# A hybrid encoder block on one core: the order of the first products, of the latent projections and of the retention output

## The chip, the cores and the metric

The kernel runs on one core of one Trainium2 chip. The metric is device time of that core in microseconds (us); lower is better. The time before is the median of three runs.

## The reference, cut to what matters

One encoder layer over 1024 tokens and 16 learned meta tokens, width 1024, all in float32:

```python
u    = rmsnorm(h)
proj = u @ w_in    # rq, rk (512 each), rv, rg (1024 each), a_cq (384), a_ckv (256), a_kr (32), two gates (1024 each)
y_ret = (silu(rg) * group_norm(bidir_retention(rope(rq), rope(rk), rv))) @ w_ret_out      # 8 heads
y_mla = attention(rmsnorm(a_cq) @ w_uq, rmsnorm(a_ckv) @ w_uk, ..w_uv, rope(a_kr)) @ w_mla_out
h = h + (sigmoid(g1) * y_ret + sigmoid(g2) * y_mla) @ w_o
h = h + (silu(n @ w_gate) * (n @ w_up)) @ w_down     # n = rmsnorm(h)
out = rmsnorm(h)[:, 16:]
```

The retention of a head works on chunks of 128 tokens: scores inside a chunk times a decay mask, a state that runs from chunk to chunk (one forward, one backward), and a group norm over the head's 128 outputs.

## The kernel before, in words

**Products.** Activations lie transposed, channels on partitions and tokens along the free axis. A 256-column slice of a projection is made by `seven` (L175), which splits weights and tokens in two halves each and forms a 2 by 2 block product with seven products instead of eight. Their names are 11, t2, t3, n1, 21, t4, 22 (L30). The contraction of 1024 channels goes in four pairs of 128-row blocks, so one product is 4 pairs x 3 matmuls = 12 matmuls of 128x512, and a `seven` has 84. There are three matmuls per pair because every fp32 operand is cut into a high and a low fp32r half, and high x high, high x low and low x high are summed (L208, L209). ScalarE writes the high half (L201 for weights, L260 and L266 for tokens), VectorE the low half (L202, L261, L267). `seven` loads the four weight blocks (L181), GpSimd adds them up (L183 to L185, L199). Products 11 and 21 share PSUM bank a, t3 and t4 bank c, n1 and 22 bank d (L31). `seven_out` (L221) drains the banks into four output blocks.

**The order.** The program is traced in the order of its text, and a scheduler lays out every engine's queue, all DMA triggers on SyncE's (SP's), by a timeline of its own; an instruction can stand in its queue before one that comes earlier in the text. A tile waits until the slot, or the closed pool's memory, that it takes over is free. On the chip each queue runs in order.

**Stage 1, the first products (L286 to L330).** For each of four pairs q the x blocks are loaded, their token blocks derived (L308 VectorE, L310 and L312 GpSimd) and split, and two slices (rg, numbers 0 and 1: `pa`, `pb`) take three or four products of that pair at once. Then x21 comes, t4 (L325) and 22 follow, and both slices are drained. The meta tokens' blocks `um`, `umd` are made after that (L333 to L342).

**Stage 2 (L481 to L492).** Four slices of v (each transposed per chunk, L436), the squares of x for the norm (`squares`, L372, GpSimd adds L380), `input_norm`, `decays` (a 128x128 decay mask per head and row weights, kept in SBUF, L358 to L360), four slices of q and k with rotary tables.

**Stage 3, the retention heads (L498 to L613).** `core_pair` loads and transposes k for two heads (L507). `core` loads v (L522), computes the states (L530 to L542) and then, for one half of the tokens after the other, scores (L552), mask (L554), output y (L558, L559), statistics (L564, L565), a square root on ScalarE (L566), the normalised y (L570), its transpose (L573), the gate (L574) and a store to DRAM tensor `z_d` (L575). Nearly all of a head's tiles have one buffer, PSUM pool `pc` has three banks. After each head a filler, one `seven`, is traced: rg slices 2 and 3, then eight gate slices; two are left after the last head. `z_sums` (L578) makes the derived blocks of `z_d` per pair, reading and writing DRAM.

**Stage 4, latents and the retention output (L614 to L758).** `cc.close()` frees the heads' memory. In it lie the latents `cq`, `ckv` (L618, L619), which stay in SBUF until the attention uses them. `latent_part` (L625) fills them from slices 20 (kv), 21 (q) and 22 (q and rotary key). Then 28 token blocks of Z are loaded from `z_d` and split (L706 to L710), the rotary parts of q are made (L720 to L746), and four slices of the retention output follow (`ret_post`, L748, L758). Attention (from L761), the output projection and the feed-forward layers come after.

## Time and profile before

| | |
|---|---|
| runs, median (lowest to highest) | 1871.55 us (1870.2 to 1873.42) |
| profiled execution, its own time | 1871.53 us |
| its span, first to last instruction | 1869.8 us |
| mean granted TensorE clock | 0.968 |
| DMA | 225.20 MB, 120 GB/s over the span |
| busy: TensorE, VectorE, ScalarE, GpSimd | 1746.0, 1337.9, 902.5, 859.9 us |

The profile is that of one execution. A group of instructions has a line number of the kernel, an engine (PE is TensorE, PEld its weight loads, DVE VectorE, ACT ScalarE, POOL GpSimd, SPq the queue that issues DMAs), the tiles written and read, a count, busy time and mean duration, and behind the second bar the idle time just before its instructions with what ended it. In a line of a timeline the first number is the start, the second the length in us. Matmuls are pipelined: the distance from start to start is what one costs, not its duration. A table of windows gives, for each stretch, its length, then busy time and count of each engine, the granted clock, the busy share of the DMA engines and GB/s.

### The profile page before, as it was taken

The numbers are of one execution on the slowest core, as the hardware profiler recorded it, in microseconds if no ns is written. First come the engines' busy times: TensorE is split into PE (matmuls) and PEld (weight loads), VectorE is DVE, ScalarE is ACT, GpSimd is POOL, SyncE is SP. The second block draws the span as 40 slices with busy tenths as digits, with TensorE's granted clock in tenths as the row PEclk, the third lists the DMA queues.
The fourth block names the chain that finished last, engine by engine and source line by source line (L and its number), as shares of the span: only waits on it lengthen the run. The fifth ranks groups of instructions, "written<-read, shape, count | busy, mean of one in ns | idle before, by whom it ended". The sixth has DMA issues, their size and how long they took to land.

```text
span 1869.8 us, 26307 instructions
## 1 busy us (share of the span) xinstructions
PE 1746.0 (93%) x8821; PEld 1461.1 (78%) x8821; DVE 1337.9 (72%) x2391; ACT 902.5 (48%) x1649; POOL 859.9 (46%) x680
## 2 busy tenths in 40 slices
PE   5799999999995749999999999999999999999998
PEld 3588778888884637889989888778888888777787
DVE  8544687677774676678878775876766666888975
ACT  5443663565442342367777734533323332544435
POOL 4612575675652313223432251567656676432331
PEclk8899999999997869999999999999999999999999
DMA  3622234445342165411101265432233333665422
GB/s 135 207 89 77 96 97 164 142 157 175 133 158 93 47 209 191 148 27 33 39 27 63 85 212 189 136 97 95 96 113 103 107 95 108 213 201 161 147 62 91
DMA packets 127415, 225.20 MB, mean 120 GB/s; under 512 B 16368, under 2 KB 30112, under 8 KB 127280
## 3 DMA queue, kind: packets, MB, share of 16 engines
q1 hardware_dynamic: 127280, 223.52, 36.3%
q8 instruction: 70, 1.15, 0.2%
q14 instruction: 65, 0.53, 0.1%
HBM read 158.64 MB, written 64.76 MB: 119 GB/s over the span
## 4 chain that ended last, share of the span: by engine, by line
PE 78%; DVE 10%; DMA 5%; issue 3%; ACT 2%; POOL 1%; SPq 0%; DVEq 0%; POOLq 0%; ACTq 0%
PE mm L209 51%; PE mm L129 3%; PE mm L130 3%; PE mm L131 3%; PE o L866 3%; PE t L836 2%; DVE slot L146 2%; PE s L129 1%; DVE slot L202 1%; PE s L130 1%; PE s L131 1%; DMA slot<-z_d 1%; DMA slot<-f_d 1%; DMA slot<-in_xT 1%; PE mm L552 1%
## 5 line engine op out<-in xcount | busy, mean ns | idle before, releaser
L209 PE MATMUL mm<-slot,slot 128*128 128x512 f32 x2604 | 597.2, 391 | 10.9 <-DVE slot L202 5.4
L209 PEld LDWEIGHTS mm<-slot,slot 128*128 128x128 f32 x2604 | 489.9, 189 | 117.1 <-DVE slot L202 7.8
L201 ACT CAST slot<-slot 128x512 fp32r<-128x512 f32 (+1 forms) x427 | 254.7, 599 | 471.3 <-PE mm L209 393.2
L202 DVE TENSOR_TENSOR slot<-slot,slot 128x512 fp32r<-128x512 f32 (+1 forms) x427 | 391.7, 919 | 97.8 <-ACT slot L201 89.5
L209 PE MATMUL mm<-ht,slot 128*128 128x512 f32 x648 | 224.5, 407 | 28.9 <-DVE slot L739 23.9
L209 PE MATMUL mm<-h,slot 128*128 128x512 f32 x648 | 228.1, 410 | 18.3 <-ACT slot L201 12.4
L209 PEld LDWEIGHTS mm<-ht,slot 128*128 128x128 f32 x648 | 124.7, 194 | 56.2 <-issue 28.2
L199 POOL TENSOR_TENSOR slot<-slot,slot 128x512 f32<-128x512 f32 (+1 forms) x61 | 83.3, 1365 | 178.3 <-DVE slot L202 144.8
L183 POOL TENSOR_TENSOR slot<-slot,slot 128x512 f32<-128x512 f32 (+1 forms) x61 | 84.8, 1391 | 174.0 <-DVE slot L202 50.2
L209 PEld LDWEIGHTS mm<-h,slot 128*128 128x128 f32 x648 | 125.6, 195 | 46.8 <-ACT slot L201 13.5
L209 PE MATMUL mm<-l,slot 128*128 128x512 f32 x324 | 130.8, 404 | 1.3 <-DVE l L267 1.3
L209 PE MATMUL mm<-lt,slot 128*128 128x512 f32 x324 | 129.8, 401 | 0.1
L146 DVE TENSOR_TENSOR slot<-slot,slot 128x512 fp32r<-128x512 f32 x123 | 107.4, 889 | 14.5 <-ACT slot L145 14.1
L184 POOL TENSOR_TENSOR slot<-slot,slot 128x512 f32<-128x512 f32 (+1 forms) x61 | 80.7, 1323 | 63.2 <-DVE slot L202 61.1
L826 DVE TENSOR_SCALAR_CACHE_REDUCE pr<-s,sq_c 128x384 f32<-128x384 f32 (+1 forms) x192 | 103.4, 574 | 8.8 <-PE t L844 5.4
L145 ACT CAST slot<-slot 128x512 fp32r<-128x512 f32 x123 | 74.7, 620 | 71.2 <-DMA slot<-f_d 29.3
L131 PE MATMUL mm<-slot,slot 128*128 128x512 f32 (+1 forms) x288 | 105.4, 366 | 0.0
L130 PE MATMUL mm<-slot,slot 128*128 128x512 f32 (+1 forms) x288 | 105.4, 366 | 0.0
L129 PE MATMUL mm<-slot,slot 128*128 128x512 f32 (+1 forms) x288 | 105.2, 367 | 0.0
L839 DVE TENSOR_TENSOR ptl<-t,pth 128x512 fp32r<-128x512 f32 x128 | 85.7, 685 | 21.9 <-ACT pth L838 21.2
L185 POOL TENSOR_TENSOR slot<-slot,slot 128x512 f32<-128x512 f32 (+1 forms) x61 | 87.7, 1437 | 1.8
L838 ACT CAST pth<-t 128x512 fp32r<-128x512 f32 x128 | 71.6, 579 | 24.0 <-PE t L836 23.6
(341 smaller groups left out, 3505.2 us busy)
## 6 DMA issues: line engine op xcount, KB each, us to landing
slot<-in_w_in SPq DMA_DIRECT2D x92, 256.0 KB
f_d<-slot SPq DMA_DIRECT2D x71, 256.0 KB
slot<-f_d SPq DMA_DIRECT2D x71, 256.0 KB
slot<-in_xT SPq DMA_DIRECT2D x48, 256.0 KB
slot<-z_d SPq DMA_DIRECT2D x44, 256.0 KB
slot<-in_w_g SPq DMA_DIRECT2D x44, 256.0 KB
slot<-in_w_u SPq DMA_DIRECT2D x44, 256.0 KB
slot<-in_w_dq SPq DMA_DIRECT2D x48, 192.0 KB
```

The source lines that it names most:

```text
L129: pe.matmul(ps, sh, mh, start=start, stop=False)
L130: pe.matmul(ps, sh, ml, start=False, stop=False)
L131: pe.matmul(ps, sl, mh, start=False, stop=stop)
L146: dve.tensor_sub(lo, t, f(hi))
L183: pool.tensor_add(s1, a21, a22)
L185: pool.tensor_sub(a21, a11, a21)
L199: pool.tensor_sub(s2, s2, a12)
L201: act.copy(hi, side[b])
L202: dve.tensor_sub(low, side[b], f(hi))
L209: pe.matmul(ps, sw[:, ks], sx, start=begins and q == qs[0] and i == 0, stop=q == nq - 1 and i == 2, skip_group_check=True)
L826: dve.tensor_scalar(pr[:, c], ps[:, :n], sq_c[:, qb : qb + 1], None, ALU.mult, ALU.max, accum_out=mx[:, j : j + 1])
L839: dve.tensor_sub(pt[1][d], tp, f(pt[0])[d])
```

## The change

1. The first products. Instead of two slices with pair after pair of all products, four slices (0 to 3) get products 11 and 21 first, with the first 512 tokens only. The other token blocks are made meanwhile, the sums on VectorE instead of GpSimd, in a fixed order (`issue_after`). Then `rest_out` drains slices 0 and 1 together, five products each, and slices 2 and 3 one by one; these two are no fillers any more. The four partial products wait in SBUF (`es`). The weight blocks 11 and 21 of the four slices are loaded twice.

```diff
+    t_d = mk(dram, (16, P, P), "t_d")
+    cq_d = mk(dram, (3, 2, P, S), "cq_d")
+    ckv_d = mk(dram, (2, 2, P, L), "ckv_d")
...
-        pool.tensor_sub(a21, a11, a21)
+        pool.tensor_sub(a21, a21, a11)
...
-        bt1 = sb(c1, "tokens", 4)
+        rfill = sb(right, "rfill", 1, side="right")
+        fill(rfill, 32)
+        mid = ExitStack()
+        bta = sb(mid, "tokens_a", 4, side="right")
+        mp = sb(mid, "misc", 1, side="right")
+        btb = sb(c1, "tokens_b", 4)
         wr1, ws1 = sb(c1, "w1r", 5), sb(c1, "w1s", 2)
         wh1, wl1 = sb(c1, "w1h", 3), sb(c1, "w1l", 3)
         cr = sb(c1, "c1", 6)
-        pm = sb(c1, "ps_mm", 5, space=PSUM)
-        pc = sb(c1, "ps_core", 3, space=PSUM)
+        pm = sb(c1, "ps_mm", 4, space=PSUM)
+        pc = sb(c1, "ps_core", 4, space=PSUM)
...
+        places = [bta]
+
+        def block(nm):
+            pl = places[0] if nm in ("11", "t2") else btb
+            return [mk(pl, (P, 512), t + nm, F32R) for t in "hl"]
...
+        def rest_out(group, pl):
+            for prod, e, post in group:
+                dve.tensor_add(e, prod("t2"), e)
+            vs = [slot(pl) for _ in group]
+            for (prod, e, post), v in zip(group, vs):
+                dve.tensor_sub(v, e, prod("n1"))
+            for (prod, e, post), v in zip(group, vs):
+                dve.tensor_add(v, prod("t3"), v)
+                post("22", v)
+            for prod, e, post in group:
+                t = slot(pl)
+                dve.tensor_add(t, prod("t4"), e)
+                post("21", t)
+            for prod, e, post in group:
+                dve.tensor_sub(e, e, prod("22"))
+                post("12", e)
...
         U = [{} for _ in range(4)]
+        cc, a1 = ExitStack(), ExitStack()
+        tb = sb(cc, "tables")
+        hold = sb(a1, "hold", 3)
         with ExitStack() as c2:
-            xp, hold = sb(c2, "x", 7), sb(c2, "hold", 8)
-            wf = sb(c2, "wfirst", 8)
+            xp, wf, wb = sb(c2, "x", 16), sb(c2, "wfirst", 2), sb(c2, "wfirst_r", 3)
...
-            kept = []
-            for q in range(4):
-                w1, w2 = column(C_MIX + 2 * q), column(C_MIX + 2 * q + 1)
-                x11 = xload(2 * q, 0)
-                if q == 0:
-                    pa = seven((wr1, ws1, wf, wf, pm), win(0), U)
-                x12, x22 = xload(2 * q, 1), xload(2 * q + 1, 1)
-                if q == 0:
-                    pb = seven((wr1, ws1, wh1, wl1, pc), win(1), U)
-                g12, n1, g22, t2 = slot(cr), slot(cr), slot(hold), slot(hold)
-                U[q]["11"] = bscale("11", x11, w1)
-                act.mul(g12, x12, w1)
-                dve.scalar_tensor_tensor(n1, x11, w1, g12, ALU.mult, ALU.subtract)
-                act.mul(g22, x22, w2)
-                pool.tensor_add(t2, g22, n1)
-                U[q]["t2"] = bsplit("t2", t2)
-                pool.tensor_sub(g12, g22, g12)
-                U[q]["t3"] = bsplit("t3", g12)
-                U[q]["n1"] = bsplit("n1", n1)
-                for b in NAMES[:3]:
-                    pa(b, [q])
-                    pb(b, [q])
-                pa("n1", [q])
-                kept.append((g22, t2))
-            x21 = [xload(2 * q + 1, 0) for q in range(4)]
-            for q in range(4):
-                U[q]["21"] = bscale("21", x21[q], column(C_MIX + 2 * q + 1))
-            for q in range(4):
-                g22, t2 = kept[q]
-                dve.scalar_tensor_tensor(t2, x21[q], column(C_MIX + 2 * q + 1), t2, ALU.mult, ALU.subtract)
-                U[q]["t4"] = bsplit("t4", t2)
-            for q in range(4):
-                U[q]["22"] = bsplit("22", kept[q][0])
-            seven_out(pa, cr, rg_post(0), {b: () for b in NAMES[:4]})
-            seven_out(pb, cr, rg_post(1), {b: () for b in NAMES[:3]})
...
+            def products(ps, w, b, q, begins):
+                ks = slice(q * P, q * P + P)
+                for i, (sw, sx) in enumerate(((w[0], U[q][b][0]), (w[0], U[q][b][1]), (w[1], U[q][b][0]))):
+                    pe.matmul(ps, sw[:, ks], sx, start=begins and i == 0, stop=q == 3 and i == 2, skip_group_check=True)
...
+            banks = [mk(pm, (P, 512), "mm") for _ in range(4)]
+            x11, x21, wa11, es = [], [], [], []
+            for i in range(4):
+                x11.append(xload(2 * i, 0))
+                wa11.append(wfirst(win(i)[0], wf if i == 3 else wh1, wf if i == 3 else wl1))
+                U[i]["11"] = bscale("11", x11[i], col(2 * i))
+                for q in range(i):
+                    products(banks[i], wa11[i], "11", q, q == 0)
+                for j in range(i + 1):
+                    products(banks[j], wa11[j], "11", i, i == 0)
+            for i in range(4):
+                es.append(slot(hold if i < 3 else cr))
+                act.copy(es[i], banks[i])
+                x21.append(xload(2 * i + 1, 0))
+                U[i]["21"] = bscale("21", x21[i], col(2 * i + 1))
+            x12, x22, made = [], [], []
+
+            def second(q):
+                w1, w2 = col(2 * q), col(2 * q + 1)
+                x12.append(xload(2 * q, 1))
+                x22.append(xload(2 * q + 1, 1))
+                dve.tensor_sub(x11[q], x11[q], x12[q])
+                act.mul(x22[q], x22[q], w2)
+                U[q]["n1"] = bscale("n1", x11[q], w1)
+                dve.scalar_tensor_tensor(x11[q], x11[q], w1, x22[q], ALU.mult, ALU.add)
+                hi, lo = U[q]["t2"] = block("t2")
+                made[:] = act.copy(hi, x11[q]), dve.tensor_sub(lo, x11[q], f(hi))
+
+            for i in range(4):
+                w = wfirst(win(i)[3], wh1, wl1)
+                for q in range(4):
+                    products(banks[i], w, "21", q, False)
+                rg_post(i)("11", banks[i])
+                if i in (1, 2):
+                    second(2 * i - 2)
+                    second(2 * i - 1)
+
...
+            with tc.issue_after(made[0].ins), tc.issue_after(made[1].ins):
+                for q in range(4):
+                    dve.scalar_tensor_tensor(x12[q], x12[q], col(2 * q), x22[q], ALU.mult, ALU.subtract)
+                    hi, lo = U[q]["t3"] = block("t3")
+                    made[:] = act.copy(hi, x12[q]), dve.tensor_sub(lo, x12[q], f(hi))
+            with tc.issue_after(made[0].ins), tc.issue_after(made[1].ins):
+                for q in range(4):
+                    dve.scalar_tensor_tensor(x21[q], x21[q], col(2 * q + 1), x11[q], ALU.mult, ALU.subtract)
+                    U[q]["t4"] = bsplit("t4", x21[q])
+                for q in range(4):
+                    U[q]["22"] = bsplit("22", x22[q])
+            rest_out([(seven(w7, win(0), U), es[0], rg_post(0)),
+                      (seven((wb, wf, wh1, wl1, pc), win(1), U), es[1], rg_post(1))], cr)
```

2. `squares` stand between the later first products, `input_norm` and `decays` after the first slice of v. The decay masks and row weights go to DRAM (`t_d`) and come back per pair and head. In a head the scores of both halves come first, and both halves share one round of statistics. `pm` has four PSUM banks instead of five, `pc` four instead of three.

```diff
-        project_v(0)
+        rest_out([(seven(w7, win(2), U), es[2], rg_post(2))], cr)
         squares(0)
-        project_v(1)
+        rest_out([(seven(w7, win(3), U), es[3], rg_post(3))], cr)
         squares(1)
-        project_v(2)
-        input_norm()
-        project_v(3)
-        decays()
+        for j in range(4):
+            project_v(j)
+            if j == 0:
+                input_norm()
+                decays()
...
+            tf, tbk = mk(cw, (P, P), "tf"), mk(cw, (P, P), "tbk")
+            load(tf, t_d[8 + p])
+            load(tbk, t_d[12 + p])
...
+            dmat = mk(cw, (P, P), "dmat")
+            load(dmat, t_d[hh])
...
+            aa = []
+            for g in range(2):
+                sc = mk(pc, (P, 512), "mm").rearrange("p (c i) -> p c i", i=P)
+                for c in range(4):
+                    t = slice((4 * g + c) * P, (4 * g + c + 1) * P)
+                    pe.matmul(sc[:, c, :], rk[hs, t], rq[hs, t], start=True, stop=True)
+                a = slot(ay).rearrange("p (c i) -> p c i", i=P)
+                dve.tensor_mul(a, sc, dmat.unsqueeze(1).broadcast_to([P, 4, P]))
+                aa.append(a)
...
+            ys = []
+            for g in range(2):
+                y = mk(pc, (P, 512), "mm").rearrange("p (c i) -> p c i", i=P)
+                for c in range(4):
+                    b = 4 * g + c
+                    pe.matmul(y[:, c, :], aa[g][:, c, :], v[:, b, :], start=True, stop=False)
+                    pe.matmul(y[:, c, :], qw[:, b, :], st[:, b, :], start=False, stop=True)
+                ys.append(y)
+            bn = mk(cw, (P, NB, 6), "bn")
+            mv = mk(cw, (P, NB, 2), "mv")
+            sd = mk(cw, (P, NB), "sd")
+            for c in range(NB):
+                dve.bn_stats(bn[:, c, :], ys[c // 4][:, c % 4, :])
+                dve.bn_aggr(mv[:, c, :], bn[:, c, :])
+            act.activation(sd, mv[:, :, 1], AF.Sqrt, bias=gneps_c)
+            dve.reciprocal(sd, sd)
...
+                    dve.tensor_scalar(yn[:, c, :], ys[g][:, c, :], mv[:, b, 0:1], sd[:, b : b + 1], ALU.subtract, ALU.mult)
```

3. The latents are fillers now. `latent_part` writes its halves into slots and stores them to `cq_d`, `ckv_d`; they come back during the retention output. Head 1 has no filler. Z's blocks 11 and t2 get memory that the heads leave, are split around the last two gate slices, and the rest follows. The rotary parts of q stand before the last retention slice. (`project_q`, `project_key`, `project_kv` hold the former code of stage 4, `project_gates` a gate slice.)

```diff
-        fillers = [(2, rg_post(2)), (3, rg_post(3))]
-        fillers += [(12 + i, gate_post(g_d if i < 4 else s_d, 2 * (i % 4))) for i in range(8)]
-
-        def filler():
-            if fillers:
-                i, post = fillers.pop(0)
-                seven_out(seven(w7, win(i), U), cr, post)
-
-        for p in range(4):
-            t = core_pair(p)
-            for h in range(2):
-                core(p, h, *t)
-                filler()
-            z_sums(p)
-        while fillers:
-            filler()
...
+        def latent_part(t, c, dst, col, first):
+            n = c.stop - c.start
+            hi = slot(cr, F32R)[:, :n]
...
+            lo = slot(cr)[:, :n]
+            dve.scalar_tensor_tensor(lo, t, col, f(hi), ALU.mult, ALU.subtract)
+            store(dst[0][:, c], f(hi))
+            store(dst[1][:, c], lo)
...
+        fillers = [lambda i=i: project_gates(i) for i in range(8)]
+        fillers[6:6] = [project_q, project_key, project_kv]
+        for p in range(4):
+            t = core_pair(p)
+            for h in range(2):
+                core(p, h, *t)
+                if 2 * p + h != 1:
+                    fillers.pop(0)()
+            z_sums(p)
+        while len(fillers) > 2:
+            fillers.pop(0)()
+        cc.close()
+
+
+        places[0] = sb(c1, "z_a", 4)
+        zx = ExitStack()
+        zr = sb(zx, "z_raw", 4)
+        Z = [{} for _ in range(4)]
+
+        def z_split(nm):
+            for q in range(4):
+                raw = slot(zr)
+                load(raw, z_d[q, NAMES.index(nm)])
+                Z[q][nm] = bsplit(nm, raw)
+
+        z_split("11")
+        fillers.pop(0)()
+        z_split("t2")
+        fillers.pop(0)()
+        for nm in NAMES[2:]:
+            z_split(nm)
+        zx.close()
...
+        ret_out(0)
+        ret_out(1)
+        ap = sb(right, "latent", 1, side="right")
+        cq = [(mk(ap, (P, S), f"cqh{k}", F32R), mk(ap, (P, S), f"cql{k}", F32R)) for k in range(3)]
+        ckv = [tuple(mk(ap, (P, 1152), f"ck{j}{k}", F32R)[:, :L] for j in "hl") for k in range(2)]
+        for i, (dst, src) in enumerate([(t, cq_d[k][j]) for k in range(3) for j, t in enumerate(cq[k])] + [
+                (t, ckv_d[k][j]) for k in range(2) for j, t in enumerate(ckv[k])]):
+            with tc.issue_after(issued[1 + i * 3 // 5].ins):
+                load(f(dst), src)
...
+        ret_out(2)
+        last = seven(w7, A["w_ro"][3], Z)
...
-        for j in range(4):
-            seven_out(seven(w7, A["w_ro"][j], Z), cr, ret_post(j))
+        seven_out(last, cr, ret_post(3))
```

4. The sign of block t3 is turned everywhere, on the weight side and on the token side, so that the in-place difference writes over its first operand.

204 lines of the change are left out of this document (93 added, 111 removed).

## The prediction

> **What bounds the kernel now.** I read the profile's first page, then windows cut where the stages change, then what TensorE waited for, then the timeline of the two places that stood out.
>
> ```profile
> span 1869.8 us, 26307 instructions
> PE 1746.0 (93%) x8821; PEld 1461.1 (78%) x8821; DVE 1337.9 (72%) x2391; ACT 902.5 (48%) x1649; POOL 859.9 (46%) x680
> PE   5799999999995749999999999999999999999998
> PEclk8899999999997869999999999999999999999999
> ```
> TensorE is the bound: busy 1746.0 of 1869.8 us, 123.8 idle. The slices show the idle time in two places only, the first two slices and slices 13 to 15, and there the granted clock drops too. The windows size both:
>
> ```profile
> 0.00:87.40 87.40, 53.67 (x180) 38.62 (x181) 61.98 (x71) 45.39 (x84) 49.26 (x47) 0.91 0.53 176
> 190.00:290.00 100.00, 96.98 (x463) 76.19 (x462) 76.59 (x99) 65.39 (x110) 69.01 (x45) 1.00 0.34 112
> 290.00:565.00 275.00, 275.00 (x1446) 228.95 (x1444) 201.88 (x433) 142.18 (x214) 162.79 (x113) 1.00 0.45 151
> 565.00:705.00 140.00, 83.86 (x358) 69.33 (x357) 87.20 (x175) 53.96 (x95) 37.87 (x28) 0.70 0.36 117
> 705.00:800.00 95.00, 93.62 (x434) 78.75 (x434) 62.17 (x110) 31.89 (x56) 24.82 (x19) 0.99 0.47 160
> ```
> Idle TensorE is 33.7 us in the lead (0 to 87.4) and 56.1 + 1.4 = 57.5 us from 565 to 800, that is 91 of the 123.8; the retention heads between run without a gap. What ended the idle time:
>
> ```profile
> PE mm L209 <- DVE slot L739: 24.2, 2, 23.9
> PE mm L677 <- ACT lss L629: 15.4, 1, 15.4
> PE mm L573 <- DVE slot L570: 9.4, 4, 2.4
> PE mm L214 <- DVE umd L342: 6.9, 1, 6.9
> PE mm L697 <- DVE slot L352: 3.3, 1, 3.3
> PE mm L559 <- DVE st L541: 2.3, 1, 2.3
> PE mm L558 <- DVE slot L554: 1.4, 2, 1.1
> ```
> 24.2 us are the Z split: retention matmuls wait for a bank that VectorE drains only after 28 token blocks. 15.4 us are the latents waiting for memory; the timeline shows ScalarE's first write into `ckh`:
>
> ```profile
> 612.92 0.72 ACT L626 ACTIVATE ckh<-slot,cols 128x512 fp32r<-128x512 f32 x1 [13.61 <-DMA z_d<-slot]
> 626.83 0.62 PE L209 MATMUL mm<-ht,slot 128*128 128x512 f32 x2
> 627.28 0.39 PE L209 MATMUL mm<-lt,slot 128*128 128x512 f32 x1
> 672.39 1.05 PE L209 MATMUL mm<-h,slot 128*128 128x512 f32 x2
> 673.25 0.63 PE L209 MATMUL mm<-l,slot 128*128 128x512 f32 x1
> ```
> It waits for the last `z_sums` store, because `cq` and `ckv` lie in the heads' memory. The matmul rows give the price of one from start to start: 0.45 / 2 = 0.225 us at full clock, 0.86 / 2 = 0.43 us shortly after an idle time. I use 0.228 with weight waits, so 2.7 us a product and 19.2 us a `seven`. The window with clock 0.70 lost 0.30 x 140 = 42 us of clock; if idle time counts at half (an estimate from these two prices), 28 of them fall on the idle 56 and 14 on slowed matmuls. So the middle loses 57.5 + 14 = 71.5 us.
>
> **The lead.** TensorE's work stays: 4 slices x 7 products, 12 matmuls each. When 216 matmuls (two products of four slices, five more of two) are done decides.
>
> ```profile
> 87.40:100.50 13.10, 12.24 (x42) 8.82 (x42) 0.82 0.20 63
> ```
> Work by line in the first 100 us (count, busy time, mean ns of one, idle time before):
>
> ```profile
> L261 DVE TENSOR_TENSOR lt<-slot,ht 128x512 fp32r<-128x512 f32 x12 | 8.6, 738 | 0.0
> L267 DVE SCALAR_TENSOR_TENSOR l<-slot,cols,h 128x512 fp32r<-128x512 f32 x8 | 6.9, 870 | 5.3 <-ACT h L266 5.3
> L308 DVE SCALAR_TENSOR_TENSOR slot<-slot,cols,slot 128x512 f32<-128x512 f32 x4 | 5.1, 1278 | 2.5 <-ACT slot L307 2.5
> L202 DVE TENSOR_TENSOR slot<-slot,slot 128x512 fp32r<-128x512 f32 x20 | 20.4, 1033 | 8.7 <-ACT slot L201 5.3 <-PE mm L209 3.4
> L228 DVE TENSOR_TENSOR slot<-slot,mm 128x512 f32<-128x512 f32 x3 | 2.0, 681 | 1.6 <-PE mm L209 1.6
> L183 POOL TENSOR_TENSOR slot<-slot,slot 128x512 f32<-128x512 f32 x4 | 5.5, 1375 | 10.7 <-DMA slot<-in_w_in 8.8 <-DVE slot L202 1.9
> L380 POOL TENSOR_TENSOR ss<-ss,slot 128x512 f32<-128x512 f32 x14 | 19.3, 1379 | 5.0 <-ACT slot L379 4.2
> ```
> And single instructions of the timeline:
>
> ```profile
> 5.27 0.75 DVE L267 SCALAR_TENSOR_TENSOR l<-slot,cols,h 128x512 fp32r<-128x512 f32 x1 [5.27 <-ACT h L266]
> 14.06 1.72 POOL L199 TENSOR_TENSOR slot<-slot,slot 128x512 f32<-128x512 f32 x1
> 14.57 1.76 DVE L261 TENSOR_TENSOR l<-slot,h 128x512 fp32r<-128x512 f32 x1
> 18.12 0.74 DVE L308 SCALAR_TENSOR_TENSOR slot<-slot,cols,slot 128x512 f32<-128x512 f32 x1
> 18.79 0.68 DVE L261 TENSOR_TENSOR lt<-slot,ht 128x512 fp32r<-128x512 f32 x1
> ```
> Before, 180 are done at 87.4 and 222 at 100.5 (the last window counts the product matmuls alone, in the first there are no others), so the 216th is at about 100. After, full-clock TensorE time is 216 x 0.228 = 49 us. Four products of 11 need only four x and four weight blocks, so it starts as early as now and has 96 matmuls (22 us) for which VectorE needs only 8 token and 8 weight halves. VectorE's sum until the 216th: 28 token halves, 16 sums (8 of them GpSimd's before), 18 weight halves, 10 drains, 4 small ones for the meta tokens. A row alone costs 0.68 or 0.74, beside a GpSimd add 1.76: the add ran 14.06 to 15.78, the subtraction 14.57 to 16.33, as if it had waited. Alone: 28 x 0.70 + 16 x 0.74 + 18 x 0.68 + 10 x 0.68 + 3 = 53 us. With the adds of two `seven` in its way, 8 x 1.38 = 11, it is 64; with the mean durations of the rows above (about 0.9 for token halves, 1.28, 1.03) 25 + 20 + 19 + 7 + 3 = 74. From 5.3 us, with a little idle, the 216th comes at 71 us (59 if nothing contends). Gain 29 us (41 at most). The meta blocks, for which TensorE waited 6.9 us, are inside VectorE's sum. ScalarE writes as many halves as VectorE but none of the sums, so it is not the last. Eight weight blocks more to load are DMA work in a stage where its share is 0.53.
>
> What filled the lead's idle time must now run later: 14 adds of `squares`, 19.3 us of GpSimd, fall into stages with VectorE and GpSimd at 77 and 69 us of 100 (window 190 to 290). Their 16 loads of x move with them on SP, past the weight loads of slices 2 and 3; 16 stores of masks come in behind the first slice of v. I charge 3 us (0 to 6) for all of it. The order that `issue_after` fixes makes t3's and t4's steps on ScalarE and VectorE queue behind t2's last copy; TensorE needs them only after 48 more matmuls (t2, n1 of two slices), 11 us, so it costs nothing beyond VectorE's sum.
>
> **The heads and the middle.** Eleven `seven` lie among the heads and their tail now (two rg, eight gates, kv), eleven after (eight gates, q, key, kv), and TensorE's work does not change. Four things go or move.
>
> The memory wait (15.4 us): latents leave through slots to DRAM, so they need nothing of the heads' memory. Gone; late next are Z's blocks in `z_a`, which do take that memory. The stores (two per part) go to SP between the heads' loads; its issues take that queue's time, and no engine's.
>
> The Z split (24.2 us): 28 low halves.
>
> ```profile
> L261 DVE TENSOR_TENSOR lt<-slot,ht 128x512 fp32r<-128x512 f32 x12 | 10.0, 865 | 1.0 <-ACT ht L260 1.0
> L261 DVE TENSOR_TENSOR l<-slot,h 128x512 fp32r<-128x512 f32 x12 | 8.2, 692 | 5.1 <-ACT h L260 4.8
> L202 DVE TENSOR_TENSOR slot<-slot,slot 128x512 fp32r<-128x512 f32 x81 | 82.9, 1023 | 25.6 <-ACT slot L201 23.9 <-POOL slot L593 1.4
> ```
> The first two rows hold 24 of the 28 (560 to 760), the third is the weight halves among the heads (280 to 600). The split costs 28 x 0.75 = 21 us and now lies beside gate slices. A gate's VectorE work is 7 x 1.02 + 5 x 0.68 = 10.6 us in 19.2 us of TensorE. From the last head on, key, kv, two gates and the first retention slice give TensorE 96 us and VectorE 5 x 10.6 + 21 + 20 = 94 us, the 20 being an estimate for some 28 low halves and rotary steps of the latents at 0.7. That covers it with nothing to spare: I keep 8 us (0 to 24). If the scheduler has spent the fillers earlier, the cover is gone and the 24 stay.
>
> The heads' tail (9.4 + 2.3 + 1.4 = 13.1 us): one round of statistics instead of two, scores off the chain; keep 4 (0 to 13). Small waits 3, slowed matmuls 4 of 14. The middle keeps 0 + 8 + 4 + 3 + 4 = 19 of 71.5: gain 52 (27 to 67).
>
> New costs: head 1 has no filler, so head 2's steps have only what is pulled forward: 3 us (0 to 8). The latents' way through DRAM is 10 blocks of half a megabyte; they queue on SP behind stores of the retention output, and behind them wait that output's weight and gate loads; 2 us (0 to 5), since the rotary part needs them only a slice later. The turned sign of t3 changes operands, not counts: nothing.
>
> Sum: 1871.53 (the execution's own time, equal to the median) - 29 - 52 + 3 + 3 + 2 = **1798.5 us**.
>
> **The rivals.** The heads' window again, its product matmuls alone:
>
> ```profile
> 290.00:565.00 275.00, 219.64 (x906) 165.62 (x904) 1.00 0.45 151
> ```
> *Fillers spent early.* The scheduler already runs ahead of the text: from 290 to 565 there are 906 / 84 = 10.8 `seven` where the text has traced eight fillers or fewer by then. If the last gates go the same way, Z's split has no cover: 24 us and some 6 of slow clock come back, 1828. Against it: work runs ahead when the heads are late, and a head's own steps become fewer rounds.
>
> *VectorE and GpSimd take turns in the lead.* If `squares` (19.3) and the next two slices' adds (6 x 1.38 = 8) are pulled into the lead, VectorE's 64 becomes 92 and the 216th comes at 98: the lead's gain is 2, the time 1825. The rows at 14.06 speak for it, the order of the text against it. The Trainium skill, "SBUF — State Buffer", section "Who interferes with whom", has this as its rule: a VectorE instruction with two SBUF inputs and a GpSimd instruction that reads SBUF lock each other out for a whole instruction. The two rows agree with that.
>
> *Slower: the heads' chain stretches.* Single buffers now get masks by DMA per head, both halves' y hold two of four banks, and all statistics wait for the second half.
>
> ```profile
> L531 ACT COPY st<-mm x8: 238/256/260, 292.6 to 576.3; 64x128 f32<-64x128 f32 x8
> 601.49 0.75 DVE L574 SCALAR_TENSOR_TENSOR slot<-mm,cols,slot 128x512 f32<-128x512 f32 x1 [0.57 <-PE mm L573]
> ```
> Heads start every (576.3 - 292.6) / 7 = 40.5 us, the last takes 26. The 906 product matmuls of the dense window cost 206 us, leaving 69 for seven heads, 10 each; all heads and eleven fillers are 291 us. At 48 us a head they last 7 x 48 + 26 = 362, 71 idle, then 30 of Z uncovered and 20 of slow clock: 121 instead of 71.5. With the lead's net gain of 21 that is 1900. It decides from about 44 us a head. Against it: the bare last head runs its halves one after the other, and the change merges them.
>
> *The scheduler gives the old order back:* 1868 to 1875.
>
> **How the numbers follow.** Both holes mostly closed 0.63, own range 1776 to 1815; fillers spent early 0.17; turns in the lead 0.12; heads stretched 0.05; old order 0.03. A measurement tells 0.2%, 3.7 us, from no change. Faster: 0.92 with nothing of the last two; same 0.03; slower 0.05. The range must reach the two partial cases with some us of their own: 1776 to 1836; it leaves out 0.05 + 0.03 and some tenth at the ends of the others.
>
> **What would show it.** In the lead, 216 product matmuls by about 71 us (right), about 98 (turns). No wait of ScalarE on `z_d` over 10 us, no wait of TensorE over 10 us between the last head and the attention, granted clock 1.0 in all slices there. Head starts below 40 us apart; over 44 and the gain is gone. A time above 1836 would mean that a new wait, not one of these, has taken the cover.

## The result and the profile after

The changed kernel takes 1818.12 us (median of 4 runs, 1813.32 to 1821.83), the kernel before 1872.49 (4 runs, 1870.2 to 1875.05): ratio 0.9708, 95% interval 0.9681 to 0.9735. That is 54 us less, where the forecast had 73. The profiled execution took 1818.95 us, 52.6 less than that of before.

The page of the changed kernel: span, busy times, TensorE's slices and its granted clock.

```profile
span 1817.2 us, 26415 instructions
...
PE   6899999999988998899999999999999999999997
...
PEclk8989999999998999899999999999999999999998
```

The hole of slices 13 to 15 is gone; what is left are shallow dips. The windows of before, cut again from the changed kernel (columns: stretch and length; busy time and count of PE, PEld, DVE, ACT, POOL; granted clock; DMA share; GB/s):

```profile
0.00:87.40 87.40, 69.34 (x272) 55.38 (x273) 68.91 (x89) 48.84 (x90) 40.28 (x39) 0.90 0.65 217
87.40:100.50 13.10, 8.46 (x22) 5.95 (x21) 10.68 (x22) 10.26 (x28) 7.77 (x7) 0.64 0.51 157
290.00:565.00 275.00, 258.06 (x1420) 214.09 (x1418) 224.37 (x509) 137.11 (x214) 177.01 (x121) 0.98 0.51 169
565.00:705.00 140.00, 133.56 (x593) 106.80 (x593) 105.04 (x147) 60.08 (x111) 50.43 (x37) 0.99 0.70 230
```

From 565 to 705 TensorE idles 6.4 us, where it idled 56.1, at clock 0.99 instead of 0.70. Two things are new: a second hole in the lead (87.4 to 100.5: 4.6 us idle, clock 0.64), and 17 us idle from 290 to 565, where there was none. What TensorE waited for longest (line, releaser: us in total, times, longest):

```profile
PE mm L212 <- DVE slot L205: 16.5, 14, 3.8
PE mm L212 <- ACT slot L204: 11.5, 3, 7.4
PE mm L649 <- DVE slot L646: 5.5, 1, 5.5
```

The waits of 24.2 us (split of Z) and 15.4 us (latents' memory) have no successor; the longest single one is 7.4 us and lies in the lead (TensorE waits until 38.2 us for a cast of ScalarE). The heads, by the first and last start of each head's state copy (L609, was L531) and of the two last steps of each head (L650, was L574):

```profile
L609 ACT COPY st<-mm x8: 242/256/261, 322.9 to 521.6; 64x128 f32<-64x128 f32 x8
L650 DVE SCALAR_TENSOR_TENSOR slot<-mm,cols,slot x16: 732/739/751, 343.2 to 552.9; 128x512 f32<-128x512 f32 x16
```

Heads now start (521.6 - 322.9) / 7 = 28.4 us apart instead of 40.5. They begin 30 us later than before, since all four rg slices come first, and end 49 us earlier (552.9 against 601.5). The start of the attention, first before, then changed: its first key step (`kf`) and the first mixture of values (`o<-pth,vt`), each by its line's first and last start.

```profile
L797 DVE TENSOR_TENSOR kf<-t,skv_b x6: 432/546/560, 780.3 to 788.4; 64x384 f32<-64x384 f32 x4, 64x272 f32<-64x272 f32 x2
L866 PE MATMUL o<-pth,vt x256: 277/283/387, 809.3 to 1067.9; 128*128 128x256 f32 x128
```
```profile
L902 DVE TENSOR_TENSOR kf<-t,skv_b x6: 432/546/559, 719.2 to 724.9; 64x384 f32<-64x384 f32 x4, 64x272 f32<-64x272 f32 x2
L971 PE MATMUL o<-pth,vt x256: 277/283/507, 756.6 to 1015.0; 128*128 128x256 f32 x128
```

The first key step comes 61.1 us earlier, the first mixture only 52.7: from one to the other it takes 37.4 us instead of 29.0. Everything behind that keeps the 52.9 us (1015.0 against 1067.9). So 8.4 us were lost at a place that the prediction did not touch. All rows of a trace are of one execution, and the four executions of the changed kernel differ by 8.5 us; a difference of a few us between two traces is therefore a hint and not a proof.

### The profile page after: what moved, and what is told of

Same layout as the page of the kernel before. It is cut to its first block, busy times and chain, and to the rows that moved or that the text cites. A ratio compares the mean times of both kernels' runs of the same rounds, so it can differ in the third digit from the quotient of the medians.

```text
span 1817.2 us, 26415 instructions
## 1 busy us (share of the span) xinstructions
PE 1735.3 (95%) x8821; PEld 1451.4 (80%) x8821; DVE 1337.8 (74%) x2391; ACT 881.7 (49%) x1626; POOL 854.3 (47%) x673
## 4 chain that ended last, share of the span: by engine, by line
PE 51%; DVE 9%; DMA 5%; issue 3%; ACT 2%; SPq 1%; POOL 1%; DVEq 0%; ACTq 0%; POOLq 0%
PE mm L212 31%; PE o L971 3%; PE t L941 3%; PE mm L132 3%; PE mm L133 2%; PE mm L134 2%; DVE slot L149 2%; DMA slot<-z_d 1%; PE s L132 1%; DMA slot<-f_d 1%; PE s L133 1%; PE s L134 1%; DVE slot L205 1%; DMA slot<-g_d 1%; DVE pr L931 1%
## 5 line engine op out<-in xcount | busy, mean ns | idle before, releaser
L204 ACT CAST slot<-slot 128x512 fp32r<-128x512 f32 (+1 forms) x419 | 249.3, 598 | 442.4 <-PE mm L212 359.0
L205 DVE TENSOR_TENSOR slot<-slot,slot 128x512 fp32r<-128x512 f32 (+1 forms) x419 | 382.9, 915 | 101.3 <-ACT slot L204 91.9
L212 PE MATMUL mm<-h,slot 128*128 128x512 f32 x584 | 200.2, 403 | 7.6 <-ACT slot L228 4.0
L186 POOL TENSOR_TENSOR slot<-slot,slot 128x512 f32<-128x512 f32 (+1 forms) x61 | 85.8, 1406 | 191.1 <-DVE slot L205 55.8
L202 POOL TENSOR_TENSOR slot<-slot,slot 128x512 f32<-128x512 f32 (+1 forms) x61 | 85.7, 1406 | 171.7 <-DVE slot L205 149.5
L212 PEld LDWEIGHTS mm<-ht,slot 128*128 128x128 f32 x648 | 123.2, 193 | 43.4 <-ACT slot L204 12.8
L212 PEld LDWEIGHTS mm<-h,slot 128*128 128x128 f32 x584 | 109.8, 190 | 31.4 <-DVE slot L205 5.0
L149 DVE TENSOR_TENSOR slot<-slot,slot 128x512 fp32r<-128x512 f32 x131 | 113.7, 883 | 17.2 <-ACT slot L148 16.8
L212 PE MATMUL mm<-l,slot 128*128 128x512 f32 x292 | 116.2, 398 | 0.0
L148 ACT CAST slot<-slot 128x512 fp32r<-128x512 f32 x131 | 79.6, 620 | 73.3 <-DMA slot<-f_d 29.5
L187 POOL TENSOR_TENSOR slot<-slot,slot 128x512 f32<-128x512 f32 (+1 forms) x61 | 82.0, 1344 | 54.8 <-DVE slot L205 52.2
L188 POOL TENSOR_TENSOR slot<-slot,slot 128x512 f32<-128x512 f32 (+1 forms) x61 | 90.5, 1484 | 1.5
```

Of the source, the lines that this page charges most:

```text
L149: dve.tensor_sub(lo, t, f(hi))
L186: pool.tensor_add(s1, a21, a22)
L188: pool.tensor_sub(a21, a21, a11)
L202: pool.tensor_sub(s2, s2, a12)
L204: act.copy(hi, side[b])
L205: dve.tensor_sub(low, side[b], f(hi))
```

## Theories

*A, the prediction's:* the lead gives 26 net, the middle 47, and both come from covering: latents that need nothing of the heads' memory, gates that lie beside the split of Z, and a little (9 us) from one round of statistics in the last head. Whatever is missing is then the lead's second hole and the attention's start. *B, the rival that stood last for experiment 5 and that its result put first:* the heads' distance sets the middle. In the kernel before TensorE is busy throughout the heads only because gates are pulled forward, and when the last head ends, nothing is left to cover what follows.

| kernel | median us | ratio to before | 95% interval | heads apart, last step us |
|---|---|---|---|---|
| before | 1872.49 | | | 40.5, 601.5 |
| changed | 1818.12 | 0.9708 | 0.9681 to 0.9735 | 28.4, 552.9 |
| 1 masks held | 1813.08 | 0.9687 | 0.9662 to 0.9711 | 28.2, 551.1 |
| 2 value weight first | 1814.72 | 0.9691 | 0.9676 to 0.9706 | 28.6, 554.5 |
| 3 both | 1809.36 | 0.9656 | 0.9641 to 0.9672 | 28.2, 550.8 |
| 4 gates written first | 1820.66 | 0.9720 | 0.9699 to 0.9740 | 28.8, 556.9 |
| 5 heads by halves | 1871.13 | 0.9998 | 0.9984 to 1.0012 | 36.9, 604.8 |
| 6 no lead sums | 1807.34 | 0.9654 | 0.9629 to 0.9678 | 28.2, 540.5 |
| 7 old lead | 1823.26 | 0.9726 | 0.9704 to 0.9749 | 27.9, 560.2 |
| 8 split held | 1829.23 | 0.9767 | 0.9753 to 0.9782 | 28.2, 550.3 |
| 9 four edits | 1808.77 | 0.9658 | 0.9643 to 0.9672 | 28.1, 536.2 |
| 10 scores by halves | 1813.23 | 0.9670 | 0.9648 to 0.9693 | 28.8, 551.2 |
| 11 statistics by halves | 1858.85 | 0.9924 | 0.9908 to 0.9940 | 35.6, 598.4 |
| 12 before, heads' edit alone | 1832.36 | 0.9784 | 0.9769 to 0.9800 | 33.8, 558.2 |

Edits 1 to 11 are made to the changed kernel, edit 12 to the kernel before. Each ratio goes by runs of the kernel before that were made beside the experiment's own, so it is not exactly the quotient of the medians shown. The last column is worked out from the rows of the state copy and of the last step, as above.

## The heads: four experiments

**5, heads by halves.** Scores, output and statistics of a head go half by half again:

```diff
-            aa = []
-            for g in range(2):
-                sc = mk(pc, (P, 512), "mm").rearrange("p (c i) -> p c i", i=P)
...
             for g in range(2):
...
+                sc = mk(pc, (P, 512), "mm").rearrange("p (c i) -> p c i", i=P)
...
+                bn = mk(cw, (P, 4, 6), "bn")
+                for c in range(4):
+                    dve.bn_stats(bn[:, c, :], y[:, c, :])
```

> The changed kernel with one part undone: in the retention heads scores, output and statistics go half by half again, two rounds of statistics instead of one; everything else stays, the masks by DMA and the four banks too. Theory A (the prediction's: one round takes some 9 us from the tail of the last head, and little elsewhere, since fillers cover the other heads): 1823 to 1831 us. Rival B (the tail is set by VectorE's other work, the rounds are hidden): 1816 to 1822 us. Rival C (the chain of every head is the limit at 28 us a head): heads 32 us apart or more and 1840 us or more.

Measured: 1871.13 us. One part undone takes back the whole gain, with the new lead, the latents' way through DRAM and the gates beside the split all in place. It is rival C, and more than it had asked for: heads 36.9 us apart where it had asked for 32. The state copy of this kernel:

```profile
L600 ACT COPY st<-mm x8: 242/247/261, 318.4 to 576.9; 64x128 f32<-64x128 f32 x8
```

**10 and 11** part the edit in two. 10 puts the scores back into the loop over halves and leaves one round of statistics; 11 leaves the scores early and puts output and statistics back by halves:

```diff
+                sc = mk(pc, (P, 512), "mm").rearrange("p (c i) -> p c i", i=P)
...
-                    pe.matmul(y[:, c, :], aa[g][:, c, :], v[:, b, :], start=True, stop=False)
+                    pe.matmul(y[:, c, :], a[:, c, :], v[:, b, :], start=True, stop=False)
```
```diff
-            bn = mk(cw, (P, NB, 6), "bn")
...
+                bn = mk(cw, (P, 4, 6), "bn")
+                mv = mk(cw, (P, 4, 2), "mv")
+                sd = mk(cw, (P, 4), "sd")
```

> The changed kernel with half of the heads' edit undone: the scores and their masks are written half by half again right ahead of each half's output, the statistics stay one round. Theory D (the heads' distance, 28.4 us now and 36.9 with everything half by half, sets when the retention output can start; what counts are the rounds of statistics): 29 to 31 us a head, 1818 to 1830 us. Theory E (what counts are the scores ahead of the state chain): 34 to 37 us a head, 1850 to 1872 us.

> The other half undone: scores early as changed, output and statistics half by half. Theory D (the rounds of statistics count): 34 to 37 us a head, 1850 to 1872 us. Theory E (the scores count): 29 to 31 us a head, 1818 to 1830 us. If neither alone brings the 37 us back, both orders are needed for it and each shows a part.

Measured: 10 gives 1813.23 us, no slower than the changed kernel (the intervals overlap), so moving the scores ahead brought nothing that these runs can show. 11 gives 1858.85, 41 us more. Theory D is right in both, though 10 came out a little below its range. The scores count only where the rounds are two: 5, which has both by halves, takes 12 us more than 11 (intervals apart). How the loss comes about is read from the product matmuls alone, cut at 320, 510 and 600 us, first of the changed kernel and then of experiment 11 (busy time, count, clock, DMA share, GB/s):

```profile
320.00:510.00 190.00, 132.57 (x523) 0.99 0.53 180
510.00:600.00 90.00, 61.52 (x240) 0.94 0.48 151
```
```profile
320.00:510.00 190.00, 141.66 (x593) 0.99 0.50 166
510.00:600.00 90.00, 9.43 (x21) 0.54 0.31 102
```

Until 510 us the kernel with the longer chain does *more* products, 593 against 523, and TensorE is as busy as in the other. Gates that were meant for later heads fill in while the heads lag. Then the gates are gone and the last heads run almost bare: 21 product matmuls in 90 us, clock 0.54. The kernel before has the same hole: 633 products from 320 to 510 us, 172 from 510 to 565 and none from 565 to 605. Its cause lies in the 200 us ahead of it, where TensorE shows hardly any idle time.

Why a head gets longer can be read in one head of experiment 11, with the two roots that ScalarE takes of the variances (`sd`) and the start of the second half's output (L630):

```profile
450.77 0.30 ACT L638 ACTIVATE sd<-mv,gneps 128x4 f32<-128x4 f32 x1
454.27 0.39 PE L630 MATMUL mm<-v,slot 128*128 128x128 f32 x2
459.51 0.30 ACT L638 ACTIVATE sd<-mv,gneps 128x4 f32<-128x4 f32 x1
```

In all eight heads the second half's output starts only when the first half's transposes have begun (here at 454.16 us), so the second half goes through output, statistics, root and normalisation after the first, and the second root comes 6.9 to 12.4 us behind the first. The changed kernel has one root a head. What a round also costs is seen at ScalarE, which waits in its queue for VectorE's statistics (`mv`), with the casts of the next products' weights behind it. ScalarE's waits among the heads, of before, of the changed kernel and of experiment 11:

```profile
ACT sd L566 <- DVE mv L565: 26.3, 10, 8.4
```
```profile
ACT sd L635 <- DVE mv L634: 8.8, 6, 2.9
```
```profile
ACT sd L638 <- DVE mv L637: 35.8, 10, 8.9
```

Sixteen rounds instead of eight cost ScalarE 18 to 27 us of waiting at this place. Its idle time in all is hardly larger, though (busy 135.2 of 280 us from 320 to 600 us, 138.1 in the changed kernel), so the wait by itself need not be the price. Which of the three stretches a head by 7 us, the order of the second half's output, ScalarE's wait or the single buffers `bn`, `mv` and `sd` between the halves, was not tried apart.

**12, the heads' edit alone,** in the kernel before, with its lead, its latents in the heads' memory and its late split:

```diff
+            ys = []
+            for g in range(2):
...
+            for c in range(NB):
+                dve.bn_stats(bn[:, c, :], ys[c // 4][:, c % 4, :])
...
-                for c in range(4):
-                    dve.bn_stats(bn[:, c, :], y[:, c, :])
```

> The kernel before with the heads' edit alone: scores early, one round of statistics, masks still in tables, three banks for the heads. Theory F (the heads' shorter chain is the cause of the middle's gain by itself): heads 30 us apart or less, 1815 to 1835 us. Theory G (it only pays together with the latents as fillers and their way through DRAM, since in the kernel before the latents wait for the heads' memory and nothing is left to cover the split): the heads end earlier, but the latents and the split still stand alone: 1850 to 1868 us.

Measured: 1832.36 us, 40 us of the 54 (theory F, at the far end of its range; its 30 us a head did not come, they are 33.8). What takes the heads from 33.8 to 28.4 us in the changed kernel (a fourth bank, masks by DMA, other fillers) no run parts. Its heads, its stretch from 565 to 705 us, and its waits of TensorE from 560 us on:

```profile
L540 ACT COPY st<-mm x8: 253/258/261, 295.5 to 532.1; 64x128 f32<-64x128 f32 x8
L581 DVE SCALAR_TENSOR_TENSOR slot<-mm,cols,slot x16: 734/747/752, 319.9 to 558.2; 128x512 f32<-128x512 f32 x16
```
```profile
565.00:705.00 140.00, 108.01 (x455) 86.70 (x454) 96.79 (x146) 57.78 (x105) 43.61 (x31) 0.84 0.47 151
```
```profile
PE mm L209 <- DVE slot L746: 24.7, 2, 23.5
...
PE mm L684 <- ACT lss L636: 2.2, 1, 2.2
```

The split's wait is still 24.7 us, as expected where nothing covers it. But the latents' wait for memory is 2.2 instead of 15.4 although the latents still lie in the heads' memory: with heads that end 43 us earlier, there is other work to do until the last `z_sums` store is done. The wait for memory was in the main a consequence of the late heads; the split's wait was not.

## The cover: two experiments

**4, gates written first.** All eleven fillers stand ahead of the split in the text:

```diff
-        while len(fillers) > 2:
+        while fillers:
...
-        z_split("11")
-        fillers.pop(0)()
-        z_split("t2")
-        fillers.pop(0)()
-        for nm in NAMES[2:]:
+        for nm in NAMES:
```

> The changed kernel with one part undone: no gate projection is left for after the heads; all eleven are done before the first block of the retention output is split. Theory A (the two gates cover the tail of the last head and the first splits of Z): TensorE idle between the last head and the first retention product, 12 to 25 us more than now, 1830 to 1845 us. Rival B (the last head's chain is short enough that the splits alone hide nothing, loads come at once): no more than 5 us, 1818 to 1823 us.

Measured: 1820.66, no difference. But the experiment did not do what it was meant to: ScalarE's first cast of the split started at 596.65 us, in the changed kernel at 593.87. The scheduler overlaps split and gates whichever comes first in the text, so this run says nothing on the cover.

**8, split held.** Therefore the same text, with the casts held behind the last gate's last sigmoid:

```diff
+        with tc.issue_after(gend[0].ins):
+            for nm in NAMES:
+                z_split(nm)
```

> The changed kernel with the cover taken away in earnest: all gates are done first and ScalarE's casts of the split of Z are held behind the last sigmoid of the last gate, where they begin at 594 us now, a slice and a half earlier. Theory A (the prediction's: the split costs 21 us of VectorE, of which two gates and the first slice hide all but a few): TensorE idle 12 to 24 us more between the last head and the attention and a slower clock behind it, 1832 to 1848 us. Rival B (the split keeps up with the first retention slice's products, block by block): 6 us or less, 1817 to 1824 us.

Measured: 1829.23, 11 us more, the intervals apart. It lies between the theories: a cover exists, at two thirds of the 16 us that the prediction gave it. TensorE waits longer for a bank of the first retention slice (6.9 us, 4.0 in the changed kernel), and waits for token halves come in:

```profile
PE mm L212 <- ACT slot L228: 6.9, 1, 6.9
...
PE mm L212 <- ACT h L271: 3.1, 4, 1.5
```

## The lead: three experiments

**7, old lead.** The text of the kernel before, from the first loads of x to the drains of slices 0 and 1, with t3's sign turned; slices 2 and 3 follow as whole `seven`:

```diff
-            for i in range(4):
-                x11.append(xload(2 * i, 0))
...
+                for b in NAMES[:3]:
+                    pa(b, [q])
+                    pb(b, [q])
+                pa("n1", [q])
...
-        rest_out([(seven(w7, win(2), U), es[2], rg_post(2))], cr)
+        seven_out(seven(w7, win(2), U), cr, rg_post(2))
```

> The changed kernel with the lead of the kernel before: two slices from the first tokens on, block by block, the other two as whole slices behind it; everything from the squares on as changed. Theory A (the two parts add; the lead is worth the 19 to 21 us by which equal counts of product matmuls come earlier from 150 to 290 us): 1836 to 1841 us. Rival B (the heads and the attention wait for other engines anyway and give a part back): 1822 to 1832 us. Rival C (the masks in the lead's hole cost the new lead 5 us that the old one would not pay): 1832 to 1836 us.

Measured: 1823.26, 5 us more than the changed kernel; the intervals overlap, so anything from nothing to some 10 is possible. Rival B. TensorE until 100 us, first with the old lead, then changed:

```profile
0.00:100.00 100.00, 70.30 (x242) 52.71 (x243) 69.26 (x96) 56.60 (x115) 55.04 (x51) 0.90 0.56 181
```
```profile
0.00:100.00 100.00, 77.30 (x291) 60.93 (x292) 79.13 (x110) 58.87 (x118) 47.58 (x44) 0.87 0.63 210
```

The new lead is ahead by 49 matmuls, 7.0 us of busy time. The heads' first state copy then comes 10.4 us earlier (322.9 against 333.3), the heads' last step 7.3 (552.9 against 560.2), and the first key step and the first mixture about 4:

```profile
L874 DVE TENSOR_TENSOR kf<-t,skv_b x6: 433/546/559, 723.2 to 729.0; 64x384 f32<-64x384 f32 x4, 64x272 f32<-64x272 f32 x2
L943 PE MATMUL o<-pth,vt x256: 277/283/430, 760.5 to 1019.2; 128*128 128x256 f32 x128
```

**1, masks held.** `decays()` waits on SyncE, ScalarE and VectorE for the end of the first v slice:

```diff
-                decays()
+                with tc.issue_after(vend[0].ins), tc.issue_after(vend[1].ins), tc.issue_after(vend[2].ins):
+                    decays()
```

> The changed kernel with one edit: the decay masks' instructions (their load, ScalarE exponentials, VectorE products, stores) are held behind the last instruction of the first v slice on ScalarE, VectorE and SyncE. Theory A (the second hole of the lead, 85 to 100 us, is these masks ahead of the weight casts on ScalarE): 276 products at about 88 us instead of 92.5, 4 to 7 us less in all, 1811 to 1814 us. Rival B (the hole is the squares and the two engines in turns, the masks only fill it): the hole stays, 1816 to 1820 us. Rival C (the masks cost the same where they go): no change in the total although the lead is shorter.

Measured: 1813.08, 5 us less by the medians, with overlapping intervals. The second hole is gone, but another takes its place, in which TensorE waits longest (3.7 us) for an exponential of the masks; the two stretches of the changed kernel and of this one:

```profile
80.00:100.00 20.00, 15.36 (x54) 11.66 (x53) 12.75 (x26) 14.01 (x35) 14.70 (x11) 0.78 0.59 179
140.00:150.00 10.00, 10.00 (x70) 8.78 (x71) 6.61 (x13) 6.29 (x13) 2.88 (x2) 1.00 0.23 81
```
```profile
80.00:100.00 20.00, 20.00 (x89) 16.26 (x88) 12.31 (x15) 8.14 (x14) 19.77 (x14) 1.00 0.54 186
140.00:150.00 10.00, 5.47 (x28) 4.03 (x27) 8.60 (x25) 9.71 (x32) 0.00 (x0) 0.89 0.34 100
```

The hole at 80 to 100 loses 4.6 us of idle time, 140 to 150 gains 4.5, and the heads end only 1.8 us earlier. So theory A names the hole's cause rightly, and its range holds the total, but up to the end of the heads the trace goes by rival C: the masks cost about the same where they went. The rest is gained behind the heads: the first key step comes 7.7 us earlier (711.5 against 719.2). The granted clock is 1.00 from 565 to 600 us there and 0.95 in the changed kernel. Why, and whether that is the edit's doing or the execution's, these runs do not show.

**6, no lead sums.** GpSimd's eight sums for slices 0 and 1 are left out:

```diff
+        if sums:
+            pool.tensor_add(s1, a21, a22)
...
+        else:
+            s1, s2 = a22, a11
```

> The changed kernel with GpSimd's eight sums for the first two weight blocks of the lead left out (the weight halves are then made from the loaded blocks as they are, so this part of the result is not the reference's); every other instruction stays. Theory A (VectorE and GpSimd hold each other up in the lead; six of these sums lie between 24 and 60 us and VectorE is busy there for 38.8 of 40 us): VectorE's steps from 20 to 60 us lose some 8 us, 216 product matmuls at about 68 us instead of 75, 1809 to 1813 us. Rival B (the lead is held by the order on ScalarE, casts behind the steps of t3): 1816 to 1820 us.

Measured: 1807.34, 11 us less, theory A and a little more. TensorE's wait of 7.4 us for a cast is gone. VectorE's steps for t2 and t4 in the timeline, changed kernel first (there GpSimd adds from 24.41 to 34.44 and from 40.33 us on), then without the sums:

```profile
28.12 1.77 DVE L364 SCALAR_TENSOR_TENSOR slot<-slot,cols,slot 128x512 f32<-128x512 f32 x1
29.81 1.77 DVE L366 TENSOR_TENSOR lt<-slot,ht 128x512 fp32r<-128x512 f32 x1
42.12 5.83 DVE L396 SCALAR_TENSOR_TENSOR slot<-slot,cols,slot 128x512 f32<-128x512 f32 x4
```
```profile
27.02 0.74 DVE L367 SCALAR_TENSOR_TENSOR slot<-slot,cols,slot 128x512 f32<-128x512 f32 x1
27.68 0.68 DVE L369 TENSOR_TENSOR lt<-slot,ht 128x512 fp32r<-128x512 f32 x1
37.43 2.07 DVE L399 SCALAR_TENSOR_TENSOR slot<-slot,cols,slot 128x512 f32<-128x512 f32 x3
```

The same steps take 0.74 and 0.68 us where no sum runs, 1.77 beside one. The rule that the prediction named for it (the Trainium skill, "SBUF — State Buffer", section "Who interferes with whom": a VectorE instruction with two SBUF inputs contends with a GpSimd instruction that reads SBUF) agrees with both sets of rows. The last of VectorE's steps for t4 ends 8.4 us earlier (39.50 against 47.95), the heads start 11 us earlier, and the total keeps all of it. The edit also spares the weight casts their wait for the sums; experiment 9, which keeps the sums and makes them on VectorE, speaks for the turns as the larger part, but no run parts the two cleanly.

## The attention's start, and the edits together

**2, value weight first.** The load of `w_uv` is written ahead of the first heads' loads:

```diff
+        vraw = mk(wv, (P, D), "vr")
+        load(vraw, A["w_uv"])
         w0 = heads_begin(0)
```

> The changed kernel with one edit: the load of the value weight of the attention is written ahead of the first two heads' loads of queries and keys, so that it is issued before them on SyncE. Theory A (the 8.5 us that the start of the attention is longer than in the kernel before come from this load being issued 8 us behind the first key product): value products start about 6 us earlier after the first key product, first mixture of values 4 to 8 us earlier, 1810 to 1814 us. Rival B (the stretch is long because the keys and queries themselves arrive late and the clock is low after a pause): 1817 to 1820 us, or slower, as the queries are then late.

The issue of that load on SyncE's queue, in the kernel before, in the changed one, and here:

```profile
775.60 0.38 SPq L121 DMA_DIRECT2D vr<-in_w_uv  x1
```
```profile
725.69 0.42 SPq L124 DMA_DIRECT2D vr<-in_w_uv  x1
```
```profile
720.20 0.42 SPq L988 DMA_DIRECT2D vr<-in_w_uv  x1
```

Before, the load was issued 4.7 us ahead of the first key step (780.3), in the changed kernel 6.5 us behind it (719.2), after the loads of queries and keys. Here the first mixture starts at 749.4, 31.1 us behind the first key step (718.3), instead of 37.4: 6.3 of the 8.4 us are back. Not all of it need be the load's. In that stretch TensorE idles 3.4 us here and 6.4 in the changed kernel, and the granted clock is 1.00 against 0.91. Experiment 1 has the late load with the full clock: 6.4 us idle, clock 1.00, 34.3 us. So, as an estimate from these three executions, about 3 us go with the load and about 3 with the slower clock, of which rival B had spoken. Measured: 1814.72, 3.4 us less by the medians, 6.6 by the profiled executions (1812.31 against 1818.95); the medians' intervals overlap.

**3, both,** 1 and 2 together:

> Both edits: the masks held behind the first v slice and the value weight's load ahead of the first heads' loads. If both theories A hold, their gains add, for they lie 600 us apart: 1804 to 1811 us, which is within the 20 us that the forecast had more than the result. If the attention's start takes what the lead gives (rival), no more than the better of the two alone.

Measured: 1809.36, 8.8 us less, about the sum of the two (5.0 + 3.4), and now the intervals are apart (0.9641 to 0.9672 against 0.9681 to 0.9735).

**9, four edits:** 3, the rotary keys' projection last, and the lead's sums on VectorE:

```diff
-        fillers[6:6] = [project_q, project_key, project_kv]
+        fillers[6:6] = [project_q, project_kv, project_key]
...
-            rest_out([(seven(w7, win(0), U), es[0], rg_post(0)),
+            rest_out([(seven(w7, win(0), U, eng=dve), es[0], rg_post(0)),
```

> Four edits to the changed kernel: masks held behind the first v slice, the value weight's load first, the rotary keys' projection as the last of the three latents instead of beside the last head, and the lead's first eight weight sums (two slices, the six that come at once) on VectorE instead of GpSimd. Theory (heads' chain and turns in the lead): the sums cost VectorE 6 x 0.7 = 4 us where GpSimd's had held it up for 8, so the heads start some 4 us earlier than with the first two edits alone (322.0 us there); without the key's steps the last head's wait of 5.5 us is gone and the heads end 30 us after its start or less: 1800 to 1806 us in all. Rival (VectorE's count in the lead is what matters, whoever holds it up; the last head's tail is covered): 1808 to 1814 us.

Measured: 1808.77, no better than 3; the rival's range holds it. Both edits did their work where they were made: the heads start at 317.4 us and end at 536.2, 4.6 and 14.6 us earlier than in 3 (322.0 and 550.8). But the first key step comes at 714.6 against 715.3. In these two traces an earlier end of the heads no longer brings the attention forward; TensorE has the same products to do in between. Kernels 3 and 9 beat the changed one by some 9 us.

## Why the prediction was right or wrong, point by point

Put beside the sum on record, by the first key step, the first mixture, and experiment 7 as the kernel between:

| | predicted | measured | from |
|---|---|---|---|
| lead | -26 | -4 | 723.2 to 719.2 |
| middle | -47 | -57 | 780.3 to 723.2 |
| attention's start | 0 | +8 | 29.0 to 37.4 |
| sum | -73 | -53 | 809.3 to 756.6 |

That the sum is 20 us off and not more is partly luck: the lead brought 22 us too little and the attention's start lost 8, and the middle, for other reasons than those given, brought 10 too much.

**The lead: the step "Gain 29 us" failed, in what it was taken to be worth.** The position was nearly right: 217 product matmuls at 75 us, forecast 216 at 71 (all matmuls of this row are products):

```profile
0.00:75.00 75.00, 56.94 (x217) 45.12 (x218) 62.12 (x81) 42.41 (x80) 27.96 (x31) 0.89 0.62 212
```

But 29 is the distance at one count of one kind of instruction. With the rest of the kernel the same (experiment 7), the new lead is ahead by 7.0 us of TensorE's busy time at 100 us, and by 4 at the attention. Even the equal counts of products in the two traces misled: until 290 us the changed kernel seemed 19 to 21 us ahead, because the kernel before had by then done more of the v slices' transposes and meta products, which the count leaves out (at 200 us 793 matmuls, 565 of them products; with the old lead in the new kernel 777, 605 of them products). Of the charges, "16 stores of masks come in behind the first slice of v" put the masks in the wrong place: they run from 88 us on, ahead of that slice, and make the second hole. Held back to where the prediction had them, they make another hole instead (experiment 1). The step "ScalarE writes as many halves as VectorE but none of the sums, so it is not the last" does not hold as it stands: the longest wait of the lead, 7.4 us, ends with a cast of ScalarE; without GpSimd's sums it is gone.

**VectorE and GpSimd in the lead** was rightly a cost, and its rival case, the 216th product at 98 us, did not come: VectorE was busy 62.1 of the first 75 us (row above), as the forecast's sum had it (64), and without GpSimd's sums the kernel is 11 us faster (experiment 6), the price that the sum had put on them.

**The middle: the size was nearly right, the reasons were not.** The step that failed is "the heads' tail: one round of statistics instead of two, scores off the chain; keep 4", 9 us of gain. Measured, the heads' edit alone is worth 40 us in the kernel before and 53 in the changed one; in the changed one output and statistics by halves carry it (41 us), and the scores cost nothing while the round is one and 12 us when it is two. The step above it, 15.4 us for memory, charged a consequence as a cause: the heads' edit alone takes 13 us of that wait away. The 16 us for the split had a right cause, since the split still costs 24.7 us of waiting when the heads are short (experiment 12), and were too large: the cover is worth 11. What the rest of the middle adds to the heads' edit is 1832.36 to 1823.26, 9 us; without the heads' edit all the rest, the lead included, brings nothing (experiment 5).

The prediction had the clue in hand. It noted that by 565 us 10.8 `seven` were done where the text had traced eight fillers or fewer, and made a rival of it *for the changed kernel*. It was the description of the kernel before: its heads were late, so its fillers were spent. And it took "the heads run without a gap" to mean that TensorE sets their pace.

**The rival "the heads' chain stretches"** had the mechanism with the wrong sign. Its rule, that the middle is seven times the heads' distance plus a bare end, is what experiments 5 and 11 show; its row of 40.5 us should have been asked what a *shorter* distance would give.

**New costs** (3 + 2): the heads now show 17 us of idle TensorE from 290 to 565 us. It was not tried how much of it is the head without a filler.

**The attention's start** was not in the sum at all. The cause is not that it comes forward: in experiment 5 it starts at 769.7, 50 us later than in the changed kernel, and the load is again issued 6.5 us behind the first key step and the stretch takes 36.7 us. What the changed kernel brings with it is the order on SyncE's queue, where the load of `w_uv` stands behind loads of keys and queries; by the estimate at experiment 2 it carries about 3 of the 8 us, and the slower clock about 3; the rest stays open.

**What was to show it:** no wait of ScalarE on `z_d` over 10 us (the longest is 2.0) and no TensorE wait over 10 us before the attention (the longest is 5.5): both came true. Head starts below 40 us: 28.4. Clock 1.0 in all slices there: nearly, slice 13 shows 0.8.

## What to carry to other kernels

An engine that is busy all through a stage can be busy with borrowed work: when a stage of n rounds runs beside fillers, compare the round's distance times n with the fillers' supply, and look for the price where the supply ends. Before a wait is charged to what it waits for, ask whether it would exist if the stage ahead ended on time; one run with that stage's chain shortened alone parts causes from consequences. Count a lead by the busy time of the limiting engine in kernels that differ in nothing else, and when the text around a stage is rewritten, see whether the order in which its loads are issued has changed.

## What the runs showed of the hardware

A change of ScalarE's function table takes 1.28 us as an instruction of its own, and it is issued ahead of the data: in the changed kernel's timeline one is done before VectorE's statistics have come.

```profile
510.24 1.28 ACT L635 ACT_TABLE_LOAD   x1
512.24 0.30 ACT L635 ACTIVATE sd<-mv,gneps 128x8 f32<-128x8 f32 x1 [0.72 <-DVE mv L634]
```

Among the heads (320 to 600 us, work by line: count, busy time, mean ns) the changed kernel has 14 such loads for the silu of a head's gate and 8 for the root, experiment 11 has 16 and 16:

```profile
L642 ACT ACT_TABLE_LOAD x14 | 18.0, 1283 | 0.3
L635 ACT ACT_TABLE_LOAD x8 | 10.3, 1283 | 0.1
```
```profile
L626 ACT ACT_TABLE_LOAD x16 | 20.5, 1283 | 0.3
L638 ACT ACT_TABLE_LOAD x16 | 20.5, 1283 | 0.3
```

The ten loads more, 12.8 us, come to 1.6 us of tables for each of the eight rounds more, beside the wait, in a stage where ScalarE is busy for about half of the time and looks as if it had room.
